# Grouped-query attention on one core: the first head's output product made pair by pair into two banks, and a new order for the whole kernel

## The chip, the cores and the metric

The kernel runs on one core of a Trainium2 chip. The metric is the device time of one execution in microseconds; the number to beat is the median of five runs of the kernel before, 362.23 us (361.67 to 362.38).

## The reference

For 8 batches there are 8 query heads and 2 key/value heads, each 1024 rows of 64 numbers in float32. Four query heads share one key/value head. Cut to what is computed:

```
scale = 1.0 / np.sqrt(head_dim)                       # head_dim 64
for g in range(n_kv_heads):                           # 2
    q_group = q[:, 4*g : 4*g+4]                       # (8, 4, 1024, 64)
    scores = scale * np.matmul(q_group, k_group.transpose(0, 1, 3, 2))
    attn = np.exp(scores - scores.max(-1, keepdims=True))
    attn = attn / (attn.sum(-1, keepdims=True) + 1e-08)
    output[:, 4*g : 4*g+4] = np.matmul(attn, v_group)
```

The kernel leaves out the maximum, since the scores are small, and gets the sum as a 65th column of ones beside V.

## The kernel before

A **job** is one query head of one batch, 64 jobs in all. A job has 8 **chunks** of 128 keys. For a chunk, a pair of TensorE matmuls (line 758) writes 128 x 1024 scores into one of three PSUM slots (`sp`). The two matmuls of a pair take the two halves of the queries. Then one of two engines makes the exponentials of the chunk:

- ScalarE, with one ACTIVATE that writes a `pt` tile (line 768). It does 378 of the 512 chunks.
- VectorE, for the other 134 chunks, with a first pass that frees the slot (`yt`, line 779), and then, for two chunks together (a **chain**), three or four steps: `zt` (line 786), `et` (line 793) and a product `zt*yt` (line 802). In most chains GpSimd takes 320 of every 1024 columns of the product (line 732), so VectorE's product is narrow there (1408 columns of two chunks in place of 2048). The exponential is the sum of `et` and `zt`. In most heads that sum is not formed: the output product takes `et` and `zt` as two terms. In the last `TAIL` heads VectorE adds them (line 807), and the chunk has one term.

The output of a job is cut into 8 **pieces** of 128 queries. A piece is a sum of 8 to 11 TensorE matmuls (line 820), each with 128 columns of a `pt`, `et` or `zt` tile as weights and 65 columns of `va` (V with its ones) as moving data. Seven pieces share a PSUM bank (`ops`). When a bank is full, VectorE takes a reciprocal of the sums (line 866) and multiplies (line 875, the norm) into `ost`, from which a job is stored to memory (line 879). The two banks are used in turn. The output of the last job is made otherwise: chunk by chunk, as its exponentials come (`pvl`, line 841).

The order of the work is written out by hand: `Plan` runs a small model of the engines with costs (`M_...`) and thresholds (`M_GAP`, `M_BACK`, `M_TOL`, `GRAIN`), chooses at each step whether TensorE makes scores for ScalarE (`A`) or for VectorE (`D`), output products (`V`, `GRAIN` matmuls at a time), idle work on a tile of zeros (`F`, line 612, called a dummy below), or waits (`W`). The kernel then issues the instructions in the order of that list. Each engine takes its own instructions in that order; the plan's times are not waited for, only data are.

V of the first key/value head is loaded by SP (line 557) and cast into `va` by GpSimd (line 560). In the kernel before, the first matmul that reads `va` is the first output product of job 0, which the plan begins when all eight chunks of job 0 have their exponentials. Q of job 1 is cast to memory by GpSimd's queue (`qd`, line 535) and read back transposed by SP's queue (`qt`, line 578).

The first chunks of job 0 go so: ScalarE takes chunks 0, 2, 3, 5, 6, 7 and VectorE takes 1 and 4. In what follows (j,c) is chunk c of job j.

Of the kernel before, what the change touches and what calls it, by code (L numbers as in the profile page):

```python
# [13 lines left out]
M_Q1 = 3400  # L14
M_QSTEP = 2700
M_WARM = 6400
M_FILL = 1e9
M_IDLE = 350
M_DUMMY = 110
# [4 lines left out]
M_MM = 30.3  # L24
M_PVTAIL = 180
# [9 lines left out]
M_GP = 850  # L35
M_GLATE = 1500

M_GAP = 120
M_RUNWAY = 1800
M_BACK = 2500  # L40
M_WAIT = 250
M_TOL = 0

HORIZON = 5500
W_A = 1.0
# [3 lines left out]
INF = float("inf")  # L49
PB = 7  # L50
NPIECE = 8
GRAIN = 2
MXD = 2
MORE = 10
TAIL = 2
GC = 320
GQ = 2
STEPS = (("zh", M_D4), ("two", M_D4), ("mul", M_D2), ("add", M_D2))
# [25 lines left out]


class State:
    LISTS = "nxt dcount pcnt pmax a_of mms slot aq dq out norms lastp".split()

    def copy(self):
        c = State.__new__(State)  # L90
# [24 lines left out]
class Plan:  # L115
# [5 lines left out]
    def __init__(self, nj, npt, nct, nyt):  # L121
        self.nj, self.npt, self.nct, self.nyt = nj, npt, nct, nyt

        self.last = (nj - 1) * NPIECE
        self.groups = [(i, min(i + PB, self.last)) for i in range(0, self.last, PB)]
        self.groups += [(self.last, self.last + NPIECE)]
        self.group_of = [g for g, (lo, hi) in enumerate(self.groups) for _ in range(lo, hi)]
        self.qready = [M_START] + [M_START + M_Q1 + M_QSTEP * j for j in range(nj - 1)]
        s = State()
        s.nxt = [0] * nj  # L130
        s.dcount = [0] * nj
        s.pcnt = [0] * nj
        s.pmax = [0] * nj
        s.a_of = [0] * nj
        s.mms = [8] * nj
        s.slot = [M_START, M_START + M_KREST, M_START + M_KREST]
        s.aq, s.dq = [], []
        s.out = [M_START, M_START]
        s.norms, s.gq = [], []
        s.tP = s.tA = M_START  # L140
        s.tD = M_START + M_SWAP
        s.tG = M_START + 9000
        s.endA, s.endD = s.tA, s.tD
        s.idleA = s.idleD = s.waste = 0
        s.mode = s.open = s.dlast = None
        s.dend = 0
        s.chains, s.heads, s.nch = [], {}, 0
        s.pc = s.done = s.a = s.used_p = s.used_c = 0
        s.lastp, s.left, s.spare = [INF] * 8, 8, None
        s.placed = 0  # L150
        s.end = False
        s.ev = []
        self.run(s)

    def ready(self, s, j, c, t):
        s.pcnt[j] += 1
        s.pmax[j] = max(s.pmax[j], t)
        if j == self.nj - 1:
            s.lastp[c] = t

    def part(self, s, ch, end):
        ch.parts -= 1
# [32 lines left out]
    def dve(self, s):  # L195
# [24 lines left out]
        elif s.norms and s.norms[0][0] <= t and s.norms[0][1] == "rec":  # L220
            _, _, lo, hi = s.norms[0]
            s.note(t, "rec", (lo, hi), None, None)
            end = t + M_REC
            s.dlast = lo
            s.norms[0] = (end, "norm", lo, hi)
        else:
            best = None
            if s.norms and s.norms[0][0] <= t:
                late = s.dlast == s.norms[0][2]
                best = (late, 5 if late else 0, None)  # L230
            for ch in s.chains:

                late = s.dlast == (ch.id, ch.at) and ch.at in (0, 3)
                key = (late, 3 - ch.at, ch)
                if best is None or key[:2] < best[:2]:
                    best = key
            if best:
                at = max(t, s.dend + M_DEP) if best[0] else t
                ch = best[2]
                if ch is None:  # L240
                    _, _, lo, hi = s.norms.pop(0)
                    s.note(t, "norm", (lo, hi), None, None)
                    end = at + M_FIX + 64 * (hi - lo) * M_D1
                    s.out[self.group_of[lo] % 2] = end + M_DTAIL + M_SEE
                    s.dlast = None
                    s.end = s.pc == self.last and not s.left and not s.norms
                else:
                    n = len(ch.pairs)
                    kind, rate = STEPS[ch.at]
                    if kind == "zh" and GC and ch.pairs[0][0] < nj - TAIL - 3 and len(s.gq) < GQ:  # L250
                        end = at + M_FIX + 1024 * n * rate
                        s.gq += [(end + M_DTAIL + M_SEE, ch, i) for i in range(n)]
                        ch.parts += n
                        ch.cols -= GC
                    cols = ch.cols if kind == "mul" else 1024
                    s.note(t, kind, None, ch.id, n, cols)
                    end = at + M_FIX + cols * n * rate
                    ch.at += 1
                    s.dlast = (ch.id, ch.at)
                    if ch.at == ch.nsteps:  # L260
                        s.chains.remove(ch)
                        self.part(s, ch, end + M_DTAIL + M_SEE)
# [14 lines left out]
        return None  # L277

    def choices(self, s):

# [18 lines left out]
        if free:  # L301
# [8 lines left out]
            elif can_a:  # L310
                full = len(free) > 1 or s.mode == "s"
                if slack <= M_GAP or (full and runway < M_RUNWAY):
                    kind = "A"
        pv = s.pc < self.last and (
            s.done > 0
            or (
                s.pcnt[s.pc // NPIECE] == 8
# [2 lines left out]
            )  # L320
        )
        wait = s.mode == "s" and any(t < x <= t + M_WAIT for x in s.slot)
        can += ["V"] * pv + ["W"] * (wait and (can_a or dj is not None))
        if kind is None:
            if wait and (dj is not None or (can_a and runway < M_RUNWAY + M_WAIT)):
                kind = "W"
            elif pv:
                kind = "V"
            elif s.left and a == nj and (free or s.spare is not None) and min(s.lastp) <= t:
                kind = "L"  # L330
            elif t < M_FILL and all(x <= t or x > t + M_IDLE for x in s.slot + [self.other(s, t)]):
                kind = "F"
            else:
                kind = "W"
        return kind, [x for x in can if x != kind]

    def other(self, s, t):

        return 0 if s.out[1 - self.group_of[s.pc] % 2] <= t else t + 1

    def turn(self, s, mode):
        if s.mode != mode:
# [4 lines left out]
    def pe(self, s, kind):  # L347
        t, nj = s.tP, self.nj
        if kind in "AD":
# [9 lines left out]
            if kind == "A":  # L359
                s.a_of[j] += 1  # L360
                s.used_p += 1
            else:
                s.dcount[j] += 1
                if j < nj - TAIL:
                    s.mms[j] += 1
        elif kind == "V":
# [8 lines left out]
            if s.done == total:  # L375
                s.done = 0
                s.pc += 1
                lo, hi = self.groups[self.group_of[s.pc - 1]]
                if s.pc == hi:
                    s.out[self.group_of[lo] % 2] = INF  # L380
                    s.norms.append((s.tP + M_PVTAIL, "rec", lo, hi))
                if s.pc % NPIECE == 0:
                    j = s.pc // NPIECE - 1
                    s.used_p -= s.a_of[j]
                    for ch in list(s.heads):
                        if j in s.heads[ch]:
                            s.heads[ch].remove(j)
                        if not s.heads[ch] and not (s.open and s.open.id == ch):
                            del s.heads[ch]
                            s.used_c -= 1  # L390
        elif kind == "L":

            if s.spare is None:
# [8 lines left out]
            if not s.left:  # L402
                s.norms.append((s.tP + M_PVTAIL, "rec", self.last, self.last + NPIECE))
        elif kind == "F":
            s.note(s.tP, "dummy", 1 - self.group_of[s.pc] % 2, None, None)
            s.tP += M_DUMMY
            s.mode = "v"
        else:
# [47 lines left out]
def kernel(  # L456
# [33 lines left out]
    dram = ctx.enter_context(tc.tile_pool(name="dram", bufs=1, space=bass.MemoryType.DRAM))  # L490
    kvp = ctx.enter_context(tc.tile_pool(name="kvp", bufs=1))
    ktp = ctx.enter_context(tc.tile_pool(name="ktp", bufs=4))
    qp = ctx.enter_context(tc.tile_pool(name="qp", bufs=10))
    vsp = ctx.enter_context(tc.tile_pool(name="vsp", bufs=2))
    pp = ctx.enter_context(tc.tile_pool(name="pp", bufs=NPT))
    yp = ctx.enter_context(tc.tile_pool(name="yp", bufs=NYT))
# [17 lines left out]
    def new_bank(i):  # L514
        ops[i] = banks[f"op{i}"].tile([128, 512], FP32, name=f"ops{i}")
        return ops[i]

    RING = PB * NPIECE
    ost = kvp.tile([128, RING, D], FP32, name="ost")
    va = kvp.tile([128, B * G, NH, 2, D + 1], BF16, name="va")  # L520
    warm = kvp.tile([128, HS], BF16, name="warm")
    ident = kvp.tile([128, 128], BF16, name="ident")
# [84 lines left out]
    new_bank(0)  # L607
    new_bank(1)

    def dummy(n, cols, bank=1):  # L610
        for _ in range(n):
            nc.tensor.matmul(  # L612
                ops[bank][:, 0:cols], lhsT=warm[:, 0:128], rhs=warm[:, 0:cols],
                start=True, stop=True,
            )

    dummy(6, HS)
# [75 lines left out]
    def flat(t):  # L693
        return t.bitcast(BF16).rearrange("p i a b -> p i (a b)")

    def terms(j, par):

        for ci in range(NC):
            c = ci if par == 0 else (ci + NH) % NC
            if (j, c) in where:  # L700
                ch, i = where[(j, c)]
# [15 lines left out]
    for when, kind, x, j, c, *cols in ev:  # L717
# [92 lines left out]
        elif kind == "pv":  # L810
            job, piece = divmod(x, NPIECE)
            b, h = divmod(job, H)
            qs, par = divmod(piece, 2)
            lo = x % PB * (D + 1)
            every = list(terms(job, par))
            if x == plan.groups[plan.group_of[x]][0] and j == 0:
                new_bank(plan.group_of[x] % 2)
            for i in range(j, j + c):
                ci, p = every[i]
# [5 lines left out]
                    stop=(i == len(every) - 1),  # L825
                )
        elif kind == "dummy":
            dummy(1, 128, x)
        elif kind == "pvl":
            b, h = divmod(NJ - 1, H)  # L830
            first = j == NC - 1
# [17 lines left out]
        elif kind in ("rec", "norm"):  # L849
            lo, hi = x  # L850
            n = hi - lo
            r = lo % RING
            if lo < plan.last:
                o = ops[plan.group_of[lo] % 2][:, 0 : n * (D + 1)]
                o = o.rearrange("p (s d) -> p s d", d=D + 1)
# [19 lines left out]
                vec = nc.vector.tensor_tensor(out=to, in0=o, in1=by, op=ALU.mult)  # L875
        elif kind == "store":
            b, h = divmod(j, H)
            r = j * NPIECE % RING
            ins = nc.sync.dma_start(
                out=rows(out[b, h], j in (0, NJ - 1)),  # L880
                in_=ost[:, r : r + NPIECE, :].rearrange("p (s two) d -> p s (two d)", two=2),
# [32 lines left out]
```

## Time and profile before

| | before |
|---|---|
| median of five runs | 362.23 us |
| the profiled execution | 362.95 us, of which the span of the core is 361.2 us |
| TensorE busy | 351.0 us (97%) |
| ScalarE busy | 351.1 us (97%) |
| VectorE busy | 347.1 us (96%) |
| GpSimd busy | 128.2 us (35%) |
| mean granted TensorE clock | 0.995 |

The profile's durations are of one execution, so sums made from them are sums against its 361.2 us. PE is TensorE's matmuls, PEld its weight loads, DVE VectorE, ACT ScalarE, POOL GpSimd, and SP the engine that issues most transfers. The share of busy time says little here, since three engines are busy 96 to 97% of the span; what decides is which engine has no gap in which stretch, and what the other two wait for there.

### The profile page before, as it was taken

What the parts mean: (1) busy time and instruction counts of PE and PEld (TensorE: products, weight loads), DVE (VectorE), ACT (ScalarE), POOL (GpSimd) and SP (SyncE); (2) the same over time, 40 slices, a digit from 0 to 9 for tenths busy, and PEclk for the clock granted to TensorE, in tenths of its full rate; (3) what the DMA queues carried; (4) which work ended last, traced back from release to release, by engine and by line L of the source; (5) the groups of instructions that cost most, each with busy time, mean ns of one, the idle gap of its engine ahead of it and who ended that gap; (6) DMA issues with size and microseconds to landing.
All of it is one profiled execution on the core that took longest, in us unless ns stands there. A gap on an engine that the chain in (4) does not pass through costs nothing.

```text
span 361.2 us, 14159 instructions
## 1 busy us (share of the span) xinstructions
PE 351.0 (97%) x6242; PEld 224.8 (62%) x6242; DVE 347.1 (96%) x491; ACT 351.1 (97%) x382; POOL 128.2 (35%) x196
## 2 busy tenths in 40 slices
PE   8789999999999999999999999999999999999995
PEld 3356666676666666666666666666656666666664
DVE  5899999999999999999999999999999999999992
ACT  5999999999999999999999999999999999999994
POOL 3144343244334454234333444334334433432000
PEclk9899999999999999999999999999999999999999
DMA  7716787475765877866477776866676455963223
GB/s 167 133 36 116 115 141 145 93 163 119 145 122 133 149 133 126 127 142 137 104 119 147 122 156 124 135 146 145 99 138 136 115 115 125 139 171 49 60 62 119
DMA packets 89406, 44.84 MB, mean 124 GB/s; under 512 B 46000, under 2 KB 87600, under 8 KB 88112
## 3 DMA queue, kind: packets, MB, share of 16 engines
q1 hardware_dynamic: 86208, 33.44, 41.4%
q0 software_dynamic: 2992, 10.23, 21.3%
q8 instruction: 49, 0.80, 1.0%
q10 hardware_dynamic: 144, 0.26, 0.3%
q14 instruction: 13, 0.11, 0.2%
HBM read 25.17 MB, written 27.00 MB: 144 GB/s over the span
## 4 chain that ended last, share of the span: by engine, by line
DVE 72%; PE 20%; DMA 3%; issue 3%; ACT 1%; DVEq 0%; POOLq 0%
DVE yt L779 34%; DVE zt L802 12%; PE ops L820 11%; PE sp L758 9%; DVE et L793 8%; DVE ost L875 8%; DVE zt L786 8%; DVE rec L866 2%; DMA qt<-qd 1%; DMA qd<-in_q_dram 1%; ACT pt L768 1%; PE sp L841 1%; PE ops L612 0%; DVEq L793 0%; POOLq L898 0%
## 5 line engine op out<-in xcount | busy, mean ns | idle before, releaser
L768 ACT ACTIVATE pt<-sp 128x1024 bf16<-128x1024 f32 x378 | 348.5, 1059 | 1.5 <-PE sp L758 1.3
L820 PE MATMUL ops<-va,pt 128*128 128x65 bf16 x2976 | 179.2, 194 | 0.0
L758 PE MATMUL sp<-qt,kt 64*128 64x512 bf16 x1024 | 173.7, 385 | 4.8 <-DMA qt<-qd 1.3
L779 DVE TENSOR_SCALAR yt<-sp 128x1024 uint16<-128x1024 f32 x134 | 162.8, 1215 | 2.1 <-PE sp L758 2.1
L820 PEld LDWEIGHTS <-pt 128*128 128x128 bf16 x2976 | 131.8, 97 | 43.7 <-issue 43.7
L820 PE MATMUL ops<-va,zt 128*128 128x65 bf16 x1056 | 127.0, 194 | 0.0
L820 PE MATMUL ops<-va,et 128*128 128x65 bf16 x1040 | 125.9, 194 | 0.0
L732 POOL TENSOR_TENSOR zt<-yt,zt 128x320 bf16<-128x320 bf16 x96 | 75.7, 789 | 121.8 <-DVE et L793 34.6
L820 PEld LDWEIGHTS <-et 128*128 128x128 bf16 x1040 | 84.3, 98 | 31.9 <-issue 31.9
L820 PEld LDWEIGHTS <-zt 128*128 128x128 bf16 x1056 | 86.2, 97 | 2.0 <-issue 2.0
L758 PEld LDWEIGHTS <-kt 64*128 64x128 bf16 x1024 | 47.1, 93 | 46.2 <-issue 23.7
L802 DVE TENSOR_TENSOR zt<-yt,zt 128x1408 bf16<-128x1408 bf16 (+1 forms) x67 | 64.8, 966 | 0.0
L535 POOL DMA_DIRECT2D qd<-in_q_dram x62 | 35.5, 573 | 38.6 <-PE sp L758 37.8
L786 DVE TENSOR_SCALAR zt<-yt 128x2048 uint16<-128x2048 uint16 x67 | 45.8, 683 | 0.5
L793 DVE TENSOR_SCALAR et<-yt 128x2048 uint16<-128x2048 uint16 x67 | 45.4, 677 | 0.0
L875 DVE TENSOR_TENSOR ost<-ops,rec 128x448 f32<-128x448 f32 x72 | 44.2, 614 | 0.3
L560 POOL CAST va<-vs 128x512 bf16<-128x512 f32 x16 | 9.8, 611 | 27.3 <-DVE et L793 10.4
L866 DVE RECIPROCAL rec<-ops 128x7 f32<-128x7 f32 x72 | 14.0, 194 | 2.1 <-PE ops L820 2.1
L543 POOL DMA_DIRECT2D kd<-in_k_dram x15 | 8.1, 540 | 12.1 <-PE sp L758 4.7
L612 PE MATMUL ops<-warm 128*128 128x128 bf16 (+1 forms) x66 | 9.6, 278 | 1.2 <-DVE warm L523 1.2
L612 PEld LDWEIGHTS <-warm 128*128 128x128 bf16 x66 | 5.0, 111 | 7.4 <-issue 6.2
L807 DVE TENSOR_TENSOR zt<-et,zt 128x2048 bf16<-128x2048 bf16 x2 | 2.4, 1216 | 0.0
(31 smaller groups left out, 15.7 us busy)
## 6 DMA issues: line engine op xcount, KB each, us to landing
out_dram<-ost SPq DMA_DIRECT2D x64, 256.0 KB, 3.1
qd<-in_q_dram POOLq DMA_DIRECT2D x63, 128.0 KB, 3.5
vs<-in_v_dram SPq DMA_DIRECT2D x16, 256.0 KB, 3.7
kd<-in_k_dram POOLq DMA_DIRECT2D x15, 128.0 KB, 3.2
kt<-kt SPq DMA_DIRECT2D x30, 64.0 KB, 2.8
qt<-qd SPq DMA_TRANSPOSE x63, 3.6
q<-in_q_dram ACTq DMA_DIRECT2D x1, 256.0 KB, 3.0
kt<-kd SPq DMA_TRANSPOSE x15, 4.2
```

The lines of the kernel that those rows point to most:

```text
L535: return nc.gpsimd.dma_start(out=t.rearrange("(a x) d -> a (x d)", x=4), in_=q[b, h].rearrange("(a x) d -> a (x d)", x=8),)
L612: nc.tensor.matmul(ops[bank][:, 0:cols], lhsT=warm[:, 0:128], rhs=warm[:, 0:cols], start=True, stop=True,)
L732: gps = nc.gpsimd.tensor_tensor(out=z, in0=flat(yt[j])[:, c, 1024 - GC :], in1=z, op=ALU.mult)
L758: now = nc.tensor.matmul(sps[x][:, half, :], lhsT=t[lo : lo + D, c // NH, ci % NH * 128 : (ci % NH + 1) * 128], rhs=qt[j][lo : lo + D, 0, ...
L768: exps.append(nc.scalar.activation(out=p, in_=where_s[(j, c)], func=AF.Exp, scale=scale))
L779: vec = nc.vector.tensor_scalar(out=yt[ch][:, i, :, :], in0=where_s[c], scalar1=EXP_A, scalar2=EXP_B, op0=ALU.mult, op1=ALU.add,)
L786: vec = nc.vector.tensor_scalar(out=zt[j][:, 0:c], in0=yt[j][:, 0:c], scalar1=0x7F, scalar2=0x3F00, op0=ALU.bitwise_and, op1=ALU.bitwise_or,)
L793: vec = ins = nc.vector.tensor_scalar(out=et[j][:, 0:c], in0=yt[j][:, 0:c], scalar1=0x7F80, scalar2=None, op0=ALU.bitwise_and,)
L802: vec = nc.vector.tensor_tensor(out=z, in0=flat(yt[j])[:, 0:c, 0 : cols[0]], in1=z, op=ALU.mult)
L820: nc.tensor.matmul(ops[plan.group_of[x] % 2][:, lo : lo + D + 1], lhsT=p[:, qs * 128 : (qs + 1) * 128], rhs=va[:, b * G + h // HPG, ci % N ...
L866: vec = nc.vector.reciprocal(out=to, in_=sums)
L875: vec = nc.vector.tensor_tensor(out=to, in0=o, in1=by, op=ALU.mult)
```

## The change

The diff, cut to its core:

```
+M_V0 = 8000
-M_GAP = 120          +M_GAP = 90
-M_BACK = 2500        +M_BACK = 3000
-M_TOL = 0            +M_TOL = 300
-GRAIN = 2            +GRAIN = 3
-TAIL = 2             +TAIL = 3
...
-        self.groups = [(i, min(i + PB, self.last)) for i in range(0, self.last, PB)]
+        self.groups = [(0, NPIECE // 2), (NPIECE // 2, NPIECE)]
+        self.groups += [(i, min(i + PB, self.last)) for i in range(NPIECE, self.last, PB)]
...
+        if j == 0:
+            s.firstp[c] = max(t, M_V0)
...
-                    if kind == "zh" and GC and ch.pairs[0][0] < nj - TAIL - 3 and len(s.gq) < GQ:
+                    if kind == "zh" and GC and ch.pairs[0][0] < nj - 5 and len(s.gq) < GQ:
...
-        pv = s.pc < self.last and (
+        pv = not s.fleft and s.pc < self.last and (
...
+        first = s.fleft and min(s.firstp) <= t
...
+            elif first:
+                kind = "E"
...
+        elif kind == "E":
+            self.turn(s, "v")
+            c = min(range(8), key=lambda c: s.firstp[c])
+            s.firstp[c] = INF
+            s.fleft -= 1
+            s.note(s.tP, "pvf", c, s.fleft, None)
+            s.tP += NPIECE * M_MM * (1 + (c in s.twice))
+            if not s.fleft:
+                s.pc = NPIECE
+                s.out = [INF, INF]
+                for lo, hi in self.groups[:2]:
+                    s.norms.append((s.tP + M_PVTAIL, "rec", lo, hi))
+                self.let_go(s, 0)
...
-    qp = ctx.enter_context(tc.tile_pool(name="qp", bufs=10))
+    qp = ctx.enter_context(tc.tile_pool(name="qp", bufs=8))
...
-    ost = kvp.tile([128, RING, D], FP32, name="ost")
+    ost = kvp.tile([128, NPIECE + RING, D], FP32, name="ost")
...
-    def dummy(n, cols, bank=1):
+    def dummy(n, cols, bank=1, beside=False):
+        lo = HS - cols if beside else 0
...
+        elif kind == "pvf":
+            first = j == NC - 1
+            if first:
+                new_bank(0)
+                new_bank(1)
+            for i in range(NPIECE):
+                par = i % 2
+                ci = x if par == 0 else (x + NH) % NC
+                every = [p for _, p in terms(0, par, [ci])]
+                lo = i % 4 * (D + 1)
+                for n, p in enumerate(every):
+                    nc.tensor.matmul(
+                        ops[i // 4][:, lo : lo + D + 1],
+                        lhsT=p[:, i // 2 * 128 : (i // 2 + 1) * 128],
+                        rhs=va[:, 0, ci % NH, ci // NH, :],
+                        start=(first and i % 4 == 0 and n == 0),
+                        stop=(j == 0 and n == len(every) - 1),
+                        skip_group_check=True,
+                    )
```

What it does:

- **Job 0, chunk by chunk.** The output of job 0 is no longer made piece by piece after its last exponential. A new event `pvf` takes one chunk and adds its term to all 8 pieces, 4 in either bank: 8 matmuls for a chunk of ScalarE, 16 for one of VectorE (two terms). The plan lets it begin at its time 8000 (`M_V0`) or when the chunk is done. The first two, for (0,0) and (0,2), stand between the scores of (0,5) and of (0,6).
- **Dummies beside.** While job 0 lies in both banks, dummies write other columns of a bank.
- **Groups.** Job 0 has two groups of 4 pieces, so all later groups of 7 are shifted, and there is one group more (74 reciprocals and 74 norms, in place of 73).
- **Tail.** Three heads, not two, get VectorE's addition: 3 additions in place of 2, and 16 output matmuls fewer.
- **Buffers.** 8 tiles for Q in place of 10; `ost` is 8 pieces larger.
- **A new plan.** With the changed thresholds the whole order is new. The counts of exponentials stay: 378 on ScalarE, 134 first passes on VectorE. Products shared with GpSimd are 45 chains in place of 48. A stretch of output products after a score occurs 244 times in place of 280.

More of the change, by code (lines that the diff above doesn't have):

```diff
@@ L36 @@
 M_GLATE = 1500
-M_GAP = 120
+M_GAP = 90
 M_RUNWAY = 1800
-M_BACK = 2500
+M_BACK = 3000
 M_WAIT = 250
-M_TOL = 0
+M_TOL = 300
 HORIZON = 5500
@@ L51 @@
 NPIECE = 8
-GRAIN = 2
+GRAIN = 3
 MXD = 2
 MORE = 10
-TAIL = 2
+TAIL = 3
 GC = 320
@@ L86 @@
 class State:
-    LISTS = "nxt dcount pcnt pmax a_of mms slot aq dq out norms lastp".split()
+    LISTS = "nxt dcount pcnt pmax a_of mms slot aq dq out norms lastp firstp twice".split()
     def copy(self):
@@ L149, in __init__ @@
         s.lastp, s.left, s.spare = [INF] * 8, 8, None
+        s.firstp, s.fleft, s.twice = [INF] * 8, 8, []
         s.placed = 0
@@ L322, in choices @@
         wait = s.mode == "s" and any(t < x <= t + M_WAIT for x in s.slot)
-        can += ["V"] * pv + ["W"] * (wait and (can_a or dj is not None))
+        first = s.fleft and min(s.firstp) <= t
+        can += ["V"] * pv + ["E"] * bool(first) + ["W"] * (wait and (can_a or dj is not None))
         if kind is None:
@@ L337, in other, with let_go @@
     def other(self, s, t):
+        if 0 < s.fleft < 8:
+            return 0
         return 0 if s.out[1 - self.group_of[s.pc] % 2] <= t else t + 1
+    def let_go(self, s, j):
+        s.used_p -= s.a_of[j]
+        for ch in list(s.heads):
+            if j in s.heads[ch]:
+                s.heads[ch].remove(j)
+            if not s.heads[ch] and not (s.open and s.open.id == ch):
+                del s.heads[ch]
+                s.used_c -= 1
     def turn(self, s, mode):
@@ L363, in pe @@
                 s.dcount[j] += 1
+                if j == 0:
+                    s.twice.append(c)
                 if j < nj - TAIL:
@@ L382, in pe @@
                 if s.pc % NPIECE == 0:
[L383 to L390, printed above, removed]
+                    self.let_go(s, s.pc // NPIECE - 1)
+        elif kind == "E":
[11 more added lines that the diff above has]
+                self.let_go(s, 0)
         elif kind == "L":
@@ L404, in pe @@
         elif kind == "F":
-            s.note(s.tP, "dummy", 1 - self.group_of[s.pc] % 2, None, None)
+            s.note(s.tP, "dummy", 1 - self.group_of[s.pc] % 2, 0 < s.fleft < 8, None)
             s.tP += M_DUMMY
@@ L518, with place_of @@
     RING = PB * NPIECE
-    ost = kvp.tile([128, RING, D], FP32, name="ost")
+    ost = kvp.tile([128, NPIECE + RING, D], FP32, name="ost")
+    def place_of(piece):
+        return piece if piece < NPIECE else NPIECE + (piece - NPIECE) % RING
     va = kvp.tile([128, B * G, NH, 2, D + 1], BF16, name="va")
@@ L608 @@
     new_bank(1)
-    def dummy(n, cols, bank=1):
+    def dummy(n, cols, bank=1, beside=False):
+        lo = HS - cols if beside else 0
         for _ in range(n):
             nc.tensor.matmul(
-                ops[bank][:, 0:cols], lhsT=warm[:, 0:128], rhs=warm[:, 0:cols],
-                start=True, stop=True,
+                ops[bank][:, lo : lo + cols], lhsT=warm[:, 0:128], rhs=warm[:, 0:cols],
+                start=not beside, stop=True, skip_group_check=beside,
             )
@@ L694, in flat, with terms @@
         return t.bitcast(BF16).rearrange("p i a b -> p i (a b)")
-    def terms(j, par):
-        for ci in range(NC):
+    def terms(j, par, only=range(NC)):
+        for ci in only:
             c = ci if par == 0 else (ci + NH) % NC
@@ L813 @@
             qs, par = divmod(piece, 2)
-            lo = x % PB * (D + 1)
+            lo = (x - plan.groups[plan.group_of[x]][0]) * (D + 1)
             every = list(terms(job, par))
-            if x == plan.groups[plan.group_of[x]][0] and j == 0:
+            if lo == j == 0:
                 new_bank(plan.group_of[x] % 2)
@@ L827 @@
         elif kind == "dummy":
-            dummy(1, 128, x)
+            dummy(1, 128, x, beside=j)
+        elif kind == "pvf":
[17 more added lines that the diff above has]
+                    )
         elif kind == "pvl":
@@ L851 @@
             n = hi - lo
-            r = lo % RING
+            r = place_of(lo)
             if lo < plan.last:
@@ L877 @@
             b, h = divmod(j, H)
-            r = j * NPIECE % RING
+            r = place_of(j * NPIECE)
             ins = nc.sync.dma_start(
```

## Prediction

> **What bounds the kernel now.** I read the chain of waits first, then the busy time by stretch, then the timeline of the first 17 us and of the last 15 us. On the page:
>
> ```profile
> PE 351.0 (97%) x6242; PEld 224.8 (62%) x6242; DVE 347.1 (96%) x491; ACT 351.1 (97%) x382; POOL 128.2 (35%) x196
> ...
> DVE 72%; PE 20%; DMA 3%; issue 3%; ACT 1%; DVEq 0%; POOLq 0%
> ```
>
> Three engines look equally full, but the chain runs over VectorE for 72% of the span. By stretch (length, then busy us of PE, PEld, DVE, ACT and POOL, granted clock, DMA):
>
> ```profile
> 5.98:9.39 3.41, 2.78 (x23) 1.17 (x19) 2.93 (x3) 3.11 (x4) 0.00 (x0) 1.00 0.92 158
> 9.39:12.80 3.41, 1.67 (x15) 0.62 (x15) 2.18 (x4) 2.81 (x4) 1.10 (x2) 1.00 0.70 113
> 12.80:16.22 3.42, 3.42 (x22) 1.59 (x19) 3.42 (x5) 3.17 (x4) 0.00 (x0) 0.50 0.79 168
> 16.22:20.00 3.78, 3.24 (x26) 1.52 (x23) 3.41 (x4) 3.78 (x5) 1.58 (x2) 1.00 0.33 74
> 20.00:345.90 325.90, 324.05 (x5881) 208.98 (x5881) 325.20 (x459) 325.76 (x355) 122.27 (x181) 1.00 0.65 125
> ```
>
> From 20 us to VectorE's last first pass VectorE is idle for 0.70 us of 325.90. So whatever VectorE loses at the start, and whatever is added to its work, reaches the end, unless less is left to do after that pass. The third row is the other thing to see: the clock is 0.50 from 12.80 to 16.22, after a stretch in which TensorE was busy 1.67 of 3.41 us. The start in order of time (start, length, engine, line):
>
> ```profile
> 6.28 4.69 ACT L768 ACTIVATE pt<-sp 128x1024 bf16<-128x1024 f32 x5 [0.49 <-PE sp L758]
> ...
> 7.35 1.31 PE L758 MATMUL sp<-qt,kt 64*128 64x512 bf16 x6 [0.36 <-ACT pt L768]
> ...
> 9.19 0.39 PE L758 MATMUL sp<-qt,kt 64*128 64x512 bf16 x2
> ...
> 10.38 0.61 POOL L560 CAST va<-vs 128x512 bf16<-128x512 f32 x1 [6.00 <-DMA vs<-in_v_dram]
> ...
> 10.92 0.61 PE L758 MATMUL sp<-qt,kt 64*128 64x512 bf16 x4 [1.34 <-DMA qt<-qd]
> ...
> 11.36 1.22 DVE L779 TENSOR_SCALAR yt<-sp 128x1024 uint16<-128x1024 f32 x1 [1.20 <-PE sp L758]
> ...
> 11.57 3.04 ACT L768 ACTIVATE pt<-sp 128x1024 bf16<-128x1024 f32 x3 [0.60 <-PE sp L758]
> ```
>
> V's cast ends at 10.38 + 0.61 = 10.99. Scores (0,3), (0,4), (0,5) end at 8.66; (0,6) is made at 9.19. At 10.92 come (1,0), which waited for the Q of job 1, and (0,7), whose Q had been there all along: it stood behind (1,0) on TensorE, and ScalarE was idle 0.60 us for it. That is the row for what a waiting matmul does to those behind it.
>
> **The new wait at the start.** The output matmuls of (0,0) and (0,2) now stand after score (0,5), and the first reads `va`. In this trace TensorE reaches it at 8.66 and can't run it before about 11.03 (10.99 and some 0.04 to be seen, as 10.92 followed 10.87). Behind it stand (0,6), (1,0), (0,7), so both ScalarE and VectorE wait.
>
> Prices from rows: output matmuls follow each other by 0.031 us (48 of line 841 took 1.66 us from 355.08), so 16 take 0.50; the step to a score 0.13 (an output matmul at 24.19, the score at 24.32); a pair of scores 0.23 (two pairs took 0.61, one 0.39), and 0.20 until its reader starts (two pairs from 10.92, reader at 11.57). An exponential takes 0.91 from start to start (12 in 11.14 us at the end). Then, after the change: output to 11.52, score (0,6) 11.62 to 11.85, its exponential at 12.05, that of (0,7) at 12.97 in place of 11.57, VectorE's pass of (1,0) at 12.29 in place of 11.36.
>
> Next the clock. TensorE now stands still from 8.66 to 11.03, and by my sums is busy about 1.7 us from 9.39 to 12.80, as before. I take the same row: 0.50 from 12.80 to 16.22. Then score (1,2) waits for the slot of (1,0) (free at 13.55) and takes 0.45 behind (1,1), so its pass starts at 14.25; the narrow product ends at 16.2. The output of (0,6) and (0,7), 16 matmuls, takes 1.0 (dummies follow each other by 0.10 there, by 0.06 at full clock, so I double 0.50), from 14.6. (1,4) follows at 15.75 to 16.2, its exponential at 16.4 where it was at 14.78. (2,0) comes after it, and its pass at 16.65. From there to the pass of (3,1) the new order has three passes of 1.13, four steps of 0.60, products of 1.13 and 0.80: 7.7 us, so 24.35, where the trace has that pass at 23.43. The work up to it is the same in both orders, so **VectorE loses 0.9 us**. With the clock full throughout, the same steps give (2,0) at 15.95 and a loss of 0.2. With half the clock already from 9.39, the first 16 matmuls and two pairs cost 0.95 more, a loss of 1.9. I take 0.9, since the stretch is as idle as the one before that the row shows.
>
> By a rule of the Trainium skill (TensorE: Matmul & The Clock Gate, Part 1: The HAM clock gate) the clock halves after at least one idle window of about 3.4 us. Taken as a window wholly idle, that would keep the clock full here, and by it the sum below would end 0.7 lower. The row stands against it: a window busy for 1.67 us was enough.
>
> ScalarE loses more, 16.4 − 14.78 = 1.6. But its 378 exponentials at 0.91 are 344 us and stretch over 349.5 (6.28 to 355.82), so it has waits in which to win back 0.7; VectorE hasn't.
>
> **VectorE's work up to its last pass**, counted in the built order of both kernels: three products full, not narrow (868 ns against 1214 in the table of groups): 3 × 0.34 = 1.0. One addition more (line 807): 1.14 (349.65 to 350.79). Two reciprocals and two norms more, of 4 pieces: between 0.3 (by width) and 0.53 for a norm, 0.11 for a reciprocal, so 0.8 to 1.3; I take 0.9. Together **3.0**, from 2.9 to 3.4.
>
> **What is left after that pass.** In the trace it starts at 345.94:
>
> ```profile
> 344.68 11.14 ACT L768 ACTIVATE pt<-sp 128x1024 bf16<-128x1024 f32 x12
> ...
> 345.94 1.21 DVE L779 TENSOR_SCALAR yt<-sp 128x1024 uint16<-128x1024 f32 x1
> ...
> 355.08 1.66 PE L841 MATMUL sp<-va,pt 128*128 128x65 bf16 x48
> ...
> 356.78 0.21 DVE L866 RECIPROCAL rec<-sp 128x8 f32<-128x8 f32 x1 [1.56 <-PE sp L841]
> ```
>
> Ten exponentials start after it; in the new order seven do. That is **−2.7** (3 × 0.91). After the last exponential (ends 355.82) TensorE still worked off output of the last job until 356.6; one chunk of 8 matmuls needs 0.25. In the new order the scores of (63,7) stand earlier, so I take **−0.25** (none to −0.5).
>
> **The rest.** Sixteen output matmuls fewer (0.5 us of TensorE) and 36 stretches fewer, each with a step of 0.13 and some 0.08 back, are 8 us of TensorE. They are hidden behind VectorE, whose gaps allow at most 0.70; I count 0, and −0.7 as an end. Uncovered they would be worth at most TensorE's 20% of the chain, 1.6. In SP's queue the store of job 0 goes ahead of the transpose of job 7's Q and could hold it, but that is asked for 11 us ahead; no cost. Eight Q tiles make a transpose wait for an earlier head, long past; none. GpSimd's 6 half products fewer (0.79 each) leave an engine that is 35% busy; none. Dummies cost nothing, being issued where TensorE has no work. The other thresholds only change the order: ±0.5.
>
> **Sum:** 0.9 + 3.0 − 2.7 − 0.25 = +0.95, say **+1.0**. The profiled span would be 362.2. The profiled execution took 362.95, 0.72 above the median of the runs, so I put the difference on the median: 362.23 + 1.0 = **363.2 us**. A measurement of this kernel tells about 0.2%, 0.7 us, from no change (its five runs span that).
>
> **Rivals.** *V is there in time* (the one that ends not slower). The timed runs were 0.7 below the profiled one, and a part may be transfers that land sooner. If V's cast ends before about 9.2, score (0,6) is still in time for ScalarE (free at 9.9), TensorE waits only for Q of job 1, and VectorE's loss falls to about 0.2: 362.4, or 361.7 if TensorE's freed time fills VectorE's gaps. For it: only the profile's own execution shows 10.99. Against it: the cast waited 6.00 us for a 256 KB load while DMA was 0.92 busy, and nothing in the change moves that.
>
> *The clock stays full*: loss 0.2, so 362.5, no change that can be told. Against it: the 0.50 row.
>
> *Half the clock twice, or new waits from the new order*: 1.0 more, 364.2, and up to 364.8 with the ±0.5. For it: TensorE now idles in two stretches running, though the first keeps some 2.2 of 3.41 us busy.
>
> *TensorE is the bound after all*: its 8 us pay 1.6, so 361.6 with the wait, and 360.7 if V is also in time. Against it: the 0.70 of 325.90.
>
> **Chances.** My sum 0.44; half clock twice or new waits 0.16; clock full 0.12; V in time 0.18 (a third of it beyond 0.2% below); TensorE the bound 0.10. Slower than 362.95: 0.60; within 0.2%: 0.23; faster than 361.5: 0.17. The range from 361.4 to 364.5 leaves out the faster half of the last two cases and the worst of the second.
>
> **What would show it.** In the changed profile: ScalarE's gap of 0.60 at 10.97 replaced by about 2.1 from 9.97, named as a wait on the scores; TensorE's first output matmul at 11.0 right after `va`'s cast; the clock 0.50 from about 12.8; VectorE's idle time still under 1 us from 20 us on; seven exponentials after its last pass. If `va` is cast before 9, or if VectorE shows several us of gaps in the middle, the reasoning is wrong.

## The result, and the profile after

The changed kernel takes **363.71 us** (median of 21 runs, 362.28 to 365.32), the kernel before 362.24 (40 runs): a ratio of 1.0043, 95% interval 1.0034 to 1.0052. It is slower by 0.43%; forecast was 363.2, slower by 0.27%. One execution of e6 (429.59 us, at clock 0.658) and one of e8 (565.39 us) are far from all the others and are left out of the times below.

The first profile of it is at odds with that: its span is 360.5 us, less than the 361.2 of before. So the page of one execution can't be set against the page of another here. The page shows first that the counts are as built:

```profile
PE 348.6 (97%) x6223; PEld 224.0 (62%) x6223; DVE 349.8 (97%) x494; ACT 351.1 (97%) x382; POOL 124.7 (35%) x190
...
DVE 70%; ACT 19%; PE 4%; issue 4%; DMA 2%; POOL 0%; DVEq 0%
```

VectorE has 2.7 us more work, TensorE 2.4 less, and TensorE's part of the chain has gone from 20% to 4%: it holds up the others less, and the kernel is not faster for it. The start of that profile in order of time (start, length, engine, line; in brackets the idle time before and who ended it):

```profile
6.39 3.77 ACT L805 ACTIVATE pt<-sp 128x1024 bf16<-128x1024 f32 x4 [0.52 <-PE sp L795]
...
9.19 0.61 POOL L596 CAST va<-vs 128x512 bf16<-128x512 f32 x1 [4.79 <-DMA vs<-in_v_dram]
...
9.85 0.66 PE L877 MATMUL ops<-va,pt 128*128 128x65 bf16 x16 [1.08 <-POOL va L596]
...
10.44 0.82 PE L795 MATMUL sp<-qt,kt 64*128 64x512 bf16 x6
```

The wait is there: TensorE stands for 1.08 us until V is cast, and the scores of (0,6), (1,0), (0,7) come behind its 16 output matmuls. But V was cast at 9.80 here, where the profile before has 10.99, and the mean granted clock of the span was 1.000. Of the 21 runs this one alone had clock 1.000, and it was the shortest. The clocks and times of the others: 0.999, five runs, 363.0 to 363.6; 0.993 to 0.995, thirteen runs, 363.5 to 364.4 (median 364.07); 0.988 and 0.989, 365.2 and 365.3. The profiled execution of before, 362.95 at 0.995, was on the contrary one of its longest.

### The profile page after: what moved, and what is told of

It is laid out like the page before. It is cut to its first block, busy times and chain, and to the rows that moved or that the text cites. A ratio compares the mean times of both kernels' runs of the same rounds, so it can differ in the third digit from the quotient of the medians.

```text
span 360.5 us, 14110 instructions
## 1 busy us (share of the span) xinstructions
PE 348.6 (97%) x6223; PEld 224.0 (62%) x6223; DVE 349.8 (97%) x494; ACT 351.1 (97%) x382; POOL 124.7 (35%) x190
## 4 chain that ended last, share of the span: by engine, by line
DVE 70%; ACT 19%; PE 4%; issue 4%; DMA 2%; POOL 0%; DVEq 0%
DVE yt L816 33%; ACT pt L805 19%; DVE zt L839 12%; DVE et L830 8%; DVE ost L931 7%; DVE zt L823 7%; DVE rec L922 2%; PE ops L857 2%; PE sp L795 2%; DMA vs<-in_v_dram 1%; DMA q<-in_q_dram 1%; PE sp L897 1%; PE ops L877 0%; POOL va L596 0%; ACT q L661 0%
## 5 line engine op out<-in xcount | busy, mean ns | idle before, releaser
L857 PE MATMUL ops<-va,pt 128*128 128x65 bf16 x2928 | 176.0, 194 | 0.0
L857 PE MATMUL ops<-va,et 128*128 128x65 bf16 x1008 | 119.4, 194 | 0.0
L769 POOL TENSOR_TENSOR zt<-yt,zt 128x320 bf16<-128x320 bf16 x90 | 71.1, 790 | 120.3 <-DVE zt L839 32.9
L857 PEld LDWEIGHTS <-et 128*128 128x128 bf16 x1008 | 81.2, 98 | 21.3 <-issue 21.0
L857 PEld LDWEIGHTS <-zt 128*128 128x128 bf16 x1040 | 84.7, 97 | 10.2 <-issue 10.2
L795 PEld LDWEIGHTS <-kt 64*128 64x128 bf16 x1024 | 48.9, 93 | 57.8 <-issue 36.6
L839 DVE TENSOR_TENSOR zt<-yt,zt 128x1408 bf16<-128x1408 bf16 (+1 forms) x67 | 66.2, 988 | 0.0
L931 DVE TENSOR_TENSOR ost<-ops,rec 128x448 f32<-128x448 f32 (+2 forms) x73 | 44.3, 607 | 0.4
L922 DVE RECIPROCAL rec<-ops 128x7 f32<-128x7 f32 (+2 forms) x73 | 14.0, 192 | 0.0
L844 DVE TENSOR_TENSOR zt<-et,zt 128x2048 bf16<-128x2048 bf16 x3 | 3.7, 1221 | 0.0
```

The source lines that it names most:

```text
L769: gps = nc.gpsimd.tensor_tensor(out=z, in0=flat(yt[j])[:, c, 1024 - GC :], in1=z, op=ALU.mult)
L795: now = nc.tensor.matmul(sps[x][:, half, :], lhsT=t[lo : lo + D, c // NH, ci % NH * 128 : (ci % NH + 1) * 128], rhs=qt[j][lo : lo + D, 0, ...
L839: vec = nc.vector.tensor_tensor(out=z, in0=flat(yt[j])[:, 0:c, 0 : cols[0]], in1=z, op=ALU.mult)
L857: nc.tensor.matmul(ops[plan.group_of[x] % 2][:, lo : lo + D + 1], lhsT=p[:, qs * 128 : (qs + 1) * 128], rhs=va[:, b * G + h // HPG, ci % N ...
L922: vec = nc.vector.reciprocal(out=to, in_=sums)
```

## The experiments

Line numbers of each profile are those of its own kernel; e1, e2 and the first profile have those of the changed kernel. Times of e1 to e11 are medians of timed runs; ratios are to the kernel before, measured on the same chip. That kernel took 362.23 us beside e1 to e4, 362.17 beside e5 to e8 and 361.94 beside e9 to e11, on three chips, so across these groups the ratios are the better measure.

### e1: the changed kernel again, for a second profile

> The changed kernel once more, unaltered, as the measure for the other three and for a second profile. Theory W (the wait for V): median about 363.7, runs spread over 2 us or more, and in this second profile the span stands above the 360.5 of the first by about as much as V's cast ends later than 9.80; with the cast at 11.0, a span of 361.5 to 362. Theory C (the clock): the span follows the granted clock, 360.5 at 1.000 and about 1 us more for each 0.005 below, wherever V's cast ends. Theory B (the body: VectorE's added work, 3.9 us between the pass of (3,1) and its last pass in the first profile): the loss is after 25 us and the start is much alike in all runs.

363.43 us, ratio 1.0037 (1.0025 to 1.0050). The second profile has a span of 361.9 at clock 0.993 and is the ordinary case:

```profile
10.02 0.61 POOL L596 CAST va<-vs 128x512 bf16<-128x512 f32 x1 [5.64 <-DMA vs<-in_v_dram]
10.69 0.66 PE L877 MATMUL ops<-va,pt 128*128 128x65 bf16 x16 [2.25 <-POOL va L596]
...
11.71 3.02 ACT L805 ACTIVATE pt<-sp 128x1024 bf16<-128x1024 f32 x3 [1.89 <-PE sp L795]
11.92 1.23 DVE L816 TENSOR_SCALAR yt<-sp 128x1024 uint16<-128x1024 f32 x1 [1.96 <-PE sp L795]
```

TensorE waits 2.25 us for V, ScalarE then 1.89 and VectorE 1.96 for the scores behind. Its chain of waits begins with the same transfer:

```profile
4.26 5.71 DMA vs<-in_v_dram
...
10.02 0.62 POOL va L596
...
10.69 0.66 PE ops L877 x16
11.34 0.79 PE sp L795 x6
```

The clock follows (by stretch: its length, then busy us of PE, PEld, DVE, ACT and POOL, then granted clock, DMA share and GB/s):

```profile
5.11:8.53 3.42, 2.93 (x28) 1.22 (x26) 2.82 (x5) 2.97 (x4) 0.00 (x0) 1.00 0.94 160
8.53:11.94 3.41, 1.25 (x22) 0.74 (x21) 1.42 (x3) 1.52 (x3) 0.61 (x1) 1.00 0.97 170
11.94:15.35 3.41, 3.41 (x41) 2.28 (x39) 3.03 (x4) 3.35 (x4) 0.49 (x1) 0.50 0.83 162
```

TensorE busy for 1.25 of 3.41 us, and the next stretch runs at 0.50. V's cast ended 0.84 later than in the first profile, and the span is 1.4 longer. Wait and clock differ together here; e4 takes them apart.

### e2: V's cast ahead of later loads

```
-            ev.append((M_START + 100, "pl", None, (b, g), None))
+            ev.append((0, "pl", None, (b, g), None))
```

> One edit: the cast of V into va stands ahead of the loads of Q of jobs 3 and 4 and of the next K in GpSimd's order, so those three loads start only when V is there and V has the transfers to itself. Theory W: V's cast ends by about 8.5, TensorE doesn't wait for it, and the median falls by 1 to 2 us to 361.7 to 362.7. Theory C: falls only as far as the clock of the runs rises to 1.0; with 0.995 it stays near 363. Theory B: 363.7 as before. If the later loads make job 3 or 4 late, ScalarE shows a gap between 18 and 30 us and it is slower.

**361.39 us**, ratio 0.9977 (0.9969 to 0.9986): 2.3 below the changed kernel, and below the kernel before. The clock was 1.000 in eight runs of eleven, never under 0.997.

```profile
6.46 8.36 ACT L805 ACTIVATE pt<-sp 128x1024 bf16<-128x1024 f32 x9 [0.45 <-PE sp L795]
...
7.49 0.61 POOL L596 CAST va<-vs 128x512 bf16<-128x512 f32 x1 [4.54 <-DMA vs<-in_v_dram]
...
8.78 0.67 PE L877 MATMUL ops<-va,pt 128*128 128x65 bf16 x16
```

V is cast at 8.10, the output matmuls run at 8.78 without a wait, and ScalarE makes nine exponentials in a row. The order of all TensorE work is that of the changed kernel, so the loss hangs on when the first loads arrive. Theory B, that the loss lies in the body, falls. The edit brings Q of job 1 sooner too: its scores stand in the four matmuls from 9.38, without a wait. Which of the two arrivals counts is what e3 tells.

### e3: the first two output steps later, V as late as it was

```
+        if e[1] == "pvf" and e[3] > NC - 3:
+            e = ((14500, 15700)[NC - 1 - e[3]],) + e[1:]
```

(and the eight steps numbered anew in their order.)

> One edit: the output of (0,0) and (0,2) is made after 13.9 and 14.7 of the plan, among the dummies there, so that scores (0,6), (1,0), (0,7) no longer stand behind it; V's load is as it was. Theory W: ScalarE's gap goes back to the 0.6 or less that Q of job 1 costs, the median falls by about 1 to 362.5 to 362.9. Theory C: TensorE stands still between 8.7 and the arrival of job 1's Q all the same, so clock and time stay, 363.5. Theory B: 363.7.

362.03 us, ratio 1.0000 (0.9989 to 1.0010), 0.5 below the range that theory W gave. The start of its profile (the line numbers are its own; 805 makes scores, 815 the exponentials):

```profile
6.32 9.27 ACT L815 ACTIVATE pt<-sp 128x1024 bf16<-128x1024 f32 x10 [0.54 <-PE sp L805]
...
9.25 0.61 POOL L596 CAST va<-vs 128x512 bf16<-128x512 f32 x1 [4.86 <-DMA vs<-in_v_dram]
...
9.81 0.73 PE L805 MATMUL sp<-qt,kt 64*128 64x512 bf16 x4 [0.19 <-DMA qt<-qd]
```

V was cast at 9.86 and no output matmul waited for it; TensorE waited 0.19 for Q of job 1, and ScalarE has no gap. So a move on TensorE alone, with the loads as they were, takes the wait and the loss away: it is V's arrival that counts, and not that of Q. TensorE was busy 2.45 of 3.41 us from 6.07 to 9.48, where e2 has 2.98 from 6.12 to 9.53. Four runs of eleven were at 0.993 to 0.995, with 362.4 to 363.2, and the seven others at 361.3 to 362.4.

### e4: TensorE kept busy while it waits

```
             if first:
+                dummy(6, HS)
                 new_bank(0)
```

> One edit: six dummies of 512 columns (about 0.21 us each at full clock) stand before the first output matmul, so TensorE works on zeros until about 10.0 where it waited for V. Theory C: all runs at clock 0.999 or more, median about 361.5 to 362.5 (the profiled execution at 1.000 had 362.28). Theory W: the wait itself is unchanged, 363.2 to 363.9. Theory B: 363.7.

363.07 us, ratio 1.0033 (1.0021 to 1.0045), far above what theory C gave and 0.1 below theory W's range. All clocks were 0.998 or more, and still it loses 0.8 to the kernel before and 1.7 to e2:

```profile
10.41 0.66 PE L878 MATMUL ops<-va,pt 128*128 128x65 bf16 x16 [0.61 <-POOL va L596]
...
11.43 3.77 ACT L805 ACTIVATE pt<-sp 128x1024 bf16<-128x1024 f32 x4 [1.65 <-PE sp L795]
```

V was cast at 10.36, ScalarE's gap is 1.65 us, and the span is 361.1 at full clock in the start, where e2 has 359.8. The wait is the larger part of the loss. The rest, some 0.4 against e1, can't be told from none by these intervals; the change's own runs, 364.07 at one halved stretch against 363.09 at 0.999, put a halved stretch at about 1.0, but they differ in V's arrival as well.

### e5, e6, e7: with V in time, the two halves of the change

All have e2's edit. e5 is the kernel before with it; e6 has the old output of job 0 with the new thresholds and three heads of additions; e7 the new output of job 0 with the thresholds and two heads of before (the five numbers below).

```
              e5, e7   e6, e2
M_GAP         120      90
M_BACK        2500     3000
M_TOL         0        300
GRAIN         2        3
TAIL          2        3
```

> The kernel before with the edit of e2 alone (V cast ahead of the later loads). What it tells: how much of e2's 361.39 belongs to the loads and not to the change. Theory L (the loads do it: Q of job 1 comes sooner too): about 361.4. Theory S (the new scheme of job 0 gains once V is there): about 362.0, since here nothing waits for V and only the wait for Q of job 1, 0.6 in the profile before, can shrink. Theory P (the new thresholds free TensorE): about 362.0 as well.

> V cast first as in e2; output of job 0 piece by piece as before; the thresholds and the additions in three heads of the change. Theory P: about 361.4, like e2. Theory S: like e5. Theory B (VectorE's added work): 0.5 to 1.0 above e5, since an addition (1.1) is added and the three exponentials fewer after the last pass pay it back only in part.

> V cast first as in e2; output of job 0 chunk by chunk as in the change; thresholds and additions (two heads) of before. Theory S: about 361.4, like e2. Theory P: about 362.0, like e5. Theory B: at or below e2, as VectorE has an addition less.

| V's cast first | old thresholds | new thresholds |
|---|---|---|
| old output of job 0 | e5 361.77, 0.9987 (0.9977 to 0.9997) | e6 361.65, 0.9984 (0.9975 to 0.9992) |
| new output of job 0 | e7 361.56, 0.9988 (0.9979 to 0.9998) | e2 361.39, 0.9977 (0.9969 to 0.9986) |

Some 0.4 of e2's 0.8 is the order of the loads, since the kernel before gains it as well (e5). The four lie within 0.4 us and their intervals overlap, so neither half of the change is shown to gain or lose once V is there; theories P and S both stay unproven at that size.

### e8: the plan told that V comes later

```
-M_V0 = 8000
+M_V0 = 11000
```

> The changed kernel with one number changed: the plan lets the output of job 0 begin at 11000, not at 8000; loads as they were. Here the first output matmuls stand behind the scores of (0,7), (1,0) and (1,1). Theory W: TensorE no longer waits for V, about 362.0 to 362.5. If the first scheme of waits is not it: 363.5.

362.64 us, ratio 1.0008 (0.9997 to 1.0018). TensorE doesn't wait for V in its profile: V is cast at 9.05, and the first output matmul is at 11.05. All clocks are 0.998 or more. It is still 0.14 above the upper end of what theory W gave: one number gives another order for all 64 jobs, and between the pass of (3,1) and the last one it takes 324.4 us for the old 322.5, with ten exponentials left as before.

### e9, e10, e11: VectorE's work in the body

All on top of e2; the second and third change the columns that GpSimd takes.

```
e9    -TAIL = 3     +TAIL = 2
e10   -GC = 320     +GC = 256
e11   -GC = 320     +GC = 384
      -M_GP = 850   +M_GP = 1000
```

> V cast first as in e2, and one number changed back: additions in the last two heads, not three (2 additions, 16 output matmuls more). If VectorE bounds the body, its last first pass comes 1.1 earlier than in e2 (348.2), and the time falls by 0 to 1.1 from 361.4, as far as ScalarE, which then has the same exponentials left, can follow. If TensorE bounds it, the 16 matmuls (0.5) make it up to 0.5 slower.

> V cast first as in e2; GpSimd takes 256 of 1024 columns in place of 320. VectorE's 46 shared products are then 1536 columns, not 1408, each 0.07 longer: 3 us more work on VectorE and nothing on the others. If VectorE bounds the body: about 2 to 3 us slower than e2, 363.4 to 364.4. If ScalarE or TensorE does: within 0.5 of 361.4.

> The other way, in search of a better version: GpSimd takes 384 columns (its cost in the plan 1000 in place of 850), VectorE's 48 shared products are 1280 columns: 3 us less and 3 narrow products more (1.0 less) on VectorE. If VectorE alone bounds the body, up to 3 faster, 358.5; but ScalarE has waits of only some 2 to 3 us to give after its start, and GpSimd's products, 0.16 longer each, hold up VectorE's where both use the memory, so 360 to 361 is likelier. If VectorE doesn't bound it: 361.4.

e9: 361.70, ratio 0.9992 (0.9980 to 1.0004). e10: 363.99, 1.0051 (1.0034 to 1.0069). e11: 362.39, 1.0006 (0.9996 to 1.0016). e10 is as VectorE's bound has it: three us more on VectorE cost 2.6 against e2. The other two are misses. e9 should have been up to 1.1 faster than e2 and came 0.3 slower, which the intervals can't tell from no change: its last pass is 3.6 earlier, not 1.1, and ten exponentials are left after it, not seven. e11 should have reached 360 to 361, and three us less on VectorE did not pay at all. In its profile VectorE's last pass is 3.6 earlier than in e2's, but twelve exponentials are left after it, not seven, and the last one starts 0.5 later (354.8 after 354.3). Up to the last pass, e2 and then e11 (length, busy us of PE, PEld, DVE, ACT and POOL, then clock and DMA):

```profile
20.00:348.20 328.20, 324.31 (x5907) 209.94 (x5907) 327.44 (x462) 327.80 (x357) 118.75 (x175) 1.00 0.66 124
20.00:344.59 324.59, 320.39 (x5803) 206.13 (x5802) 323.00 (x459) 323.80 (x352) 137.94 (x181) 1.00 0.66 125
```

In both, VectorE and ScalarE are busy but for 0.4 to 1.6 us. I read it so that the two bound the body together: what one gains the other has to follow. It is a reading and not shown, since each of these numbers also gives a new order of all the work.

## Why the prediction held, and where its terms did not

The steps of the sum, read from profiles (us; e5 and e2 are the old and the new kernel with V in time):

| | before | after, first | e1 | e5 | e2 |
|---|---|---|---|---|---|
| V cast at | 10.99 | 9.80 | 10.64 | 8.07 | 8.10 |
| pass of (3,1) starts | 23.43 | 22.50 | 23.88 | 22.23 | 21.68 |
| from there to VectorE's last pass | 322.5 | 326.4 | 326.5 | 322.5 | 326.5 |
| from there to the last exponential | 8.8 | 6.0 | 6.0 | 8.8 | 6.0 |
| from there to the end | 6.5 | 5.5 | 5.5 | 6.5 | 5.5 |
| span | 361.2 | 360.5 | 361.9 | 360.0 | 359.8 |

**The new wait: right, and it is the cause.** ScalarE's gap of "about 2.1 from 9.97" is 1.89 from 9.82 in e1 and 0.71 in the first profile; e2 and e3 take the wait away and the loss with it. My first rival, V in time, is what e2 made of it: 361.4, where I had 362.4, or 361.7 with TensorE's freed time; 0.4 of the difference the order of the loads alone gives (e5).

**VectorE's loss at the start: too large against the profile, too small against the runs.** The step said +0.9 on 23.43; e1 has +0.45. But 23.43 belongs to an execution that already had a halved stretch and a wait for Q. Against e2, with the same order and no wait, e1 loses 2.2 here.

**VectorE's work: mis-sized, 3.9 for 3.0.** The addition is 1.14 as taken. All reciprocals and norms together take 1.3 more from start to start, not 0.9, since a reciprocal directly before its norm is followed only after some 0.23, not 0.11, and e1 has eleven such in this stretch, the profile before seven. The products are 1.4 to 1.5, not 1.0:

```profile
L839 DVE TENSOR_TENSOR zt<-yt,zt 128x1408 bf16<-128x1408 bf16 x45 | 39.8, 884 | 0.0
L839 DVE TENSOR_TENSOR zt<-yt,zt 128x2048 bf16<-128x2048 bf16 x22 | 26.4, 1200 | 0.0
```

These are groups of the first profile after (busy us, mean ns): 66.2 us, where before had 41.7 + 23.1 = 64.8. A narrow product has become longer, 884 ns for 868; no run asked why.

**What is left after the last pass: right**, −2.7 predicted and measured.

**ScalarE's waits "in which to win back 0.7": wrong.** The prediction's own row from 20 us on has ScalarE busy for 325.76 of 325.90 us, more than VectorE's 325.20. ScalarE's last exponential starts at 354.7 before and at 356.4 in e1: 1.7 later, after a loss of 1.6 that the prediction gave it at the start, so nothing was won back. And the chain of e1 does not stay on VectorE, as its page shows:

```profile
DVE 69%; ACT 19%; PE 5%; issue 3%; DMA 2%; POOL 0%; DVEq 0%
```

From 288.3 to 355.6 us that chain runs over exponentials and nothing else, where the chain of before has 1% on ScalarE.
The sum by VectorE comes out all the same, as both engines have next to no gaps and end on the same exponential; busy times can't tell which of them holds the end up, but the chain of e1 names ScalarE.

**The tail: mis-sized, −0.9 for −0.25.** The end of e1:

```profile
355.67 0.91 PE L897 MATMUL sp<-va,pt 128*128 128x65 bf16 x24 [0.17 <-ACT pt L805]
...
356.92 1.01 PE L897 MATMUL sp<-va,pt 128*128 128x65 bf16 x24
...
357.97 0.21 DVE L922 RECIPROCAL rec<-sp 128x8 f32<-128x8 f32 x1 [1.47 <-PE sp L897]
358.21 0.69 DVE L931 TENSOR_TENSOR ost<-sp,rec 128x512 f32<-128x512 f32 x1
```

TensorE now waits for an exponential before the last job's output, as predicted, and the last reciprocal follows the last exponential's end (357.46) by 0.5, where it was 1.0. That is −0.45. From the last norm to the end it is 3.7, where it was 4.15: another −0.45 in the last store, whose reason no run here was made to find.

That the sum holds for e1 is luck in part: the errors are −0.45 at the start, +0.95 in VectorE's work and −0.7 in the tail, and they nearly cancel. The table gives 0.45 + 3.95 − 2.72 − 0.94 = +0.74 against the profile before, where the sum said +0.95.

**"So I put the difference on the median": the step that cost the most.** It took the profile before as an ordinary execution. Of 35 runs of before measured with e5, eight had a clock under 0.9965, with a median of 362.96; the other 27 had 361.94. The profile before, 362.95 at 0.995, was like the eight. Like against like the sum comes near: 364.07 for the changed kernel at 0.993 to 0.995 is +1.1, and 363.09 at 0.999 against 361.94 is +1.15. These runs of before are from another measurement, though; on e1's own chip the same comparison gives +0.4 (363.69 against two runs, 363.18 and 363.33) and +1.0 (363.18 against 362.19). The rest of the measured 1.5 goes with the halved stretch, which by the mean clocks came in one run of four or fewer before and in fifteen of 21 after; that the stretch costs this is argued from the clocks and not shown by an experiment.

**The clock.** The rule quoted from the Trainium skill (TensorE: Matmul & The Clock Gate, Part 1: The HAM clock gate), read as a window wholly idle, would have kept the clock full; two profiles stand against it, with 1.67 and 1.25 busy us of 3.41 before the halving, while the stretch of the first profile after with 2.22 was followed by none. Taking the row was right for e1, whose clock is 0.50 from 11.94 to 15.35.

**TensorE's freed 8 us: rightly counted as nothing.** TensorE's share of the chain fell to 4%, and the new thresholds and the third addition together moved e5 to e6 by 0.1 us. The 8 us themselves were not measured: the profile has 2.4 less of busy time, and the steps between stretches are not in it.

**The rivals.** *The clock stays full*: I had 362.5. By their mean clocks six runs of 21 had no halved stretch in the start (e4's and e8's profiles, at 0.998, have the clock halved only after 359 us). One of the six took 362.28, with V cast early; the five at 0.999 took 363.0 to 363.6, and e4 took 363.07. So a full clock alone did not bring 362.5. *Half the clock twice* fits the two at 0.988 and 0.989, 365.2 and 365.3, above the 364.8 given; no profile of such a run was had. *TensorE is the bound* had 361.6 with the wait; with the wait it was 363.7.

## What to carry to other kernels

An instruction that is moved ahead brings its data's deadline with it: before an order is changed, look up when each operand lands in the trace, and count everything that stands behind the moved instruction on its engine. Here a step that fills idle TensorE time lost 1.5 us because V was 1 to 2 us late for it, and lost nothing once V's cast stood before three loads that nobody needed yet. Then it was 0.8 below the kernel before, half of which that kernel gains from the same order of loads; a gain of the step itself is not shown. And before a sum is set on a median, look whether the profiled execution is a typical one; the granted clock of each run told it here.

## What was not expected of the hardware

- A transfer of 256 KB issued at the same place (4.29 and 4.26 us) was cast at 9.80 in one execution of the same kernel and at 10.64 in another; in e8, with the same first loads and issued at 4.42, at 9.05. With three 128 KB loads moved behind it (e2, issued at 4.42), it was cast at 8.10.
- VectorE is busy for 327.4 of the 328.2 us from 20 us to its last pass in e2. More work on it cost almost in full (e10), but less of it did not help (e11). ScalarE had no gaps either (327.8 of 328.2): an engine without a gap need not be the only bound.
